# Thirty-two experts in a fixed order: the next gate ahead of the down projection, 512-column products, 64-row combining

## The chip, the core and the metric

The kernel runs on one core of one Trainium2 chip. The metric is the device time of one execution in microseconds (us). A core has a matrix engine (TensorE; PE in the profile, its weight loads PEld), a vector engine (VectorE, DVE), a scalar engine (ScalarE, ACT), GpSimd (POOL), a queue engine that here only issues transfers (SyncE, SP) and 16 DMA engines. Every engine runs its own instructions in order and waits on semaphores for the others. Matrix products are written to PSUM (eight banks, of 512 float32 in each of 128 partitions); everything else lies in SBUF, 128 partitions wide.

## What is computed

One layer of an encoder on 256 tokens of 1024 channels: a token mixer (two kinds of attention), a normalization, a mixture of experts with the four best of 32 experts for each token, and a second normalization. The change touches the experts and the last normalization:

```python
logits = xt @ w_router + b_router
top_vals, top_idx = lax.top_k(logits, TOP_K)          # 4 of 32
gates = softmax(top_vals)
# for each expert e, on the tokens that chose it:
hcat = xb @ w_up[e] + b_up[e]                         # 1024 -> 2048
gate = min(hcat[:, :1024], 7.0)
up = clip(hcat[:, 1024:], -7.0, 7.0)
act = gate * sigmoid(1.702 * gate) * (up + 1.0)
ys = act @ w_down[e] + b_down[e]                      # 1024 -> 1024
# out[token] += gate weight * ys;  x = layer_norm(alpha * x + out, ln2_g, ln2_b)
```

All is float32. The weights of the experts are 32 x 12 MiB, and each is read once.

## The kernel before, in words

The first 230 us are the mixer, the first normalization and the router. Then come the experts. An expert has room for 64 tokens, and two experts make a pair: `gather_x` picks the tokens of a pair with 0/1 matrices (`oh`) by TensorE products (tile `px`, line 575) and copies them, transposed, to `xe` (ACT, line 577).

An expert (`expert`, lines 596 to 656) is computed in two halves of 512 hidden channels. For each half, `up(c, 0)` makes the gate products and `up(c, 1)` the up products, each into one PSUM tile `pu` of 128 x 256 (two such tiles take turns). The two 64-row halves of `pu` hold two groups of 256 columns. A product starts with the bias, two bfloat16 matmuls (line 710), then come eight steps over the 1024 input channels (line 606). VectorE limits the gate (line 613), ScalarE takes the sigmoid (615), VectorE multiplies (616), limits the up part (619) and multiplies (620). `turned` transposes the result (line 626, tile `pa`, copied by ACT at 628), and `down` (line 636) multiplies it with the down weights into `pd`, whose two 64-row halves are 512 output columns each. ACT and DVE copy one half of `pd` each (653, 655) to `y`, at the rows of the expert within the pair.

When a pair is done, `combine` (line 681) multiplies the 128 rows of `y` with the gate weights `ot` and adds to four PSUM banks `acc`. `gates_of` makes `ot` (588 to 593). `start` puts the biases of the down projection (675) and the scaled residual (676) into `acc`, during expert 0.

The weights lie in memory as pieces of 1 MiB, 12 to an expert. `load` (lines 111 to 119) takes 20 places in SBUF in turn (`SLOTS`); SP issues all the loads in one queue, and a load waits until TensorE has read the place's former piece, and by a ring of eight semaphores for the landing of an earlier load. Ten pieces are loaded while the mixer runs. The last piece is loaded in two halves. Behind it SP loads the last normalization's two rows, spread to 128 partitions by the transfer (lines 734, 735).

A scheduler of the framework decides the order on each engine before the run; the order of the code is only its input.

Of the kernel before, what the change touches and what calls it, by code (L numbers as in the profile page):

```python
# [10 lines left out]
F32 = mybir.dt.float32  # L11
# [57 lines left out]
def encoder(ctx, tc, x, xt, w_in, b_in, lam, w_pa, w_pb, w_out, b_out, ln1g, ln1b, cols, b_r, w_ex, b_up,  # L69
# [39 lines left out]
    here = {}  # L109

    def load():

        n = len(here)
        e, j, h = n // 12, n // 2 % 6, n % 2
        r = slot(SLOTS[n % len(SLOTS)])
        here[e, j, h] = part(r, 0, 2048, 4 if j < 4 else 2)
        c = 1024 if n == 12 * NE - 1 else 2048
        for i in range(0, 2048, c):
            nc.sync.dma_start(r[:, i:i + c], w_ex[e, n % 12, :, i:i + c])

    def weights(e):
        while len(here) < 12 * (e + 1):
            load()
        return lambda c, b, k: here[e, 2 * c + b, k // 4][:, k % 4], lambda c, k: here[e, 4 + c, k // 2][:, k % 2]


    with ExitStack() as c1:
# [142 lines left out]
        def softmaxes(b, c, tabs):  # L270
# [9 lines left out]
            for j in range(2):  # L280
                p = turn("p", ps_)
                for tt in range(NT):
                    i = 2 * j + tt
                    s = moe.tile([P, T], F32, name="s", tag="gc", bufs=4)
# [77 lines left out]
        lamt = moe.tile([P, 4, HD], F32, name="lamt", tag="oh")  # L362
# [201 lines left out]
    def gather_x(ps, q, pos):  # L564

        oh = moe.tile([P, NT, 2, CAP], F32, name="oh", tag="oh")
# [3 lines left out]
        xe = moe.tile([P, KD, P], F32, name="xe", tag=f"xe{q % 2}")  # L570
        for k0 in range(0, KD, 4):
            px = ps.tile([P, 4, P], F32, name="px", tag="m")
            for k in range(4):
                for tt in range(NT):
                    PE.matmul(px[:, k], x1[:, tt, (k0 + k) * P:(k0 + k + 1) * P],  # L575
                              oh[:, tt].rearrange("p a b -> p (a b)"), start=tt == 0, stop=tt == NT - 1)
            S.copy(xe[:, k0:k0 + 4], px)  # L577
        return oh, xe

    def gather(ps, q, pos, g):  # L580
        oh, xe = gather_x(ps, q, pos)
        return xe, gates_of(ps, oh, g)

    def gates_of(ps, oh, g):
# [3 lines left out]
        V.tensor_mul(og, oh, g[:, :, :, None].to_broadcast(sh))  # L588
# [7 lines left out]
    def expert(ps, xe, i, wu, wd, bias, y, after=None):  # L596

        ats = []

        def up(c, b):  # L600
            pu = ps.tile([P, 256], F32, name="pu", bufs=2)
            for h in range(2):
                bias(pu[h * CAP:(h + 1) * CAP], b * FE + c * 512 + h * 256)
# [39 lines left out]
        if after is not None:  # L643
            after()
# [212 lines left out]
```

## Time and profile before

| | |
|---|---|
| median of 3 runs | 1199.31 us (1198.02 to 1201.79) |
| the profiled execution | 1198.99 us, of which the span of its instructions is 1197.2 us |
| TensorE busy in the span | 1103.0 us (92%) |
| VectorE, ScalarE, GpSimd busy | 304.3, 214.4, 54.5 us |
| read from memory | 439.2 MB |
| mean granted clock of TensorE | 0.99 of full speed |

The span runs from the first instruction of the profiled execution to its last; 1.8 us lie around it. Busy times of different engines overlap.

### The profile page before, as it was taken

The page shows a single profiled execution, that of the slowest core. Times are in us where ns is not written, and L with a number is a line of the kernel's source. Part 1 is how long each engine was busy: PE and PEld are TensorE (multiplying, and loading weights), DVE is VectorE, ACT ScalarE, POOL GpSimd, SP SyncE. Part 2 cuts the span into 40 slices and gives each one's busy share as a digit, 9 for nine tenths or more (in the row PEclk, how much of TensorE's full clock was granted, in tenths as well). Part 3 has the DMA queues.
Part 4 walks back from the last instruction along what each step waited for, and adds up shares of the span by engine and source line. Part 5 has one row for each costly group of instructions (what it writes and reads, how often), then busy time and mean ns, then how long its engine had stood idle before and what let it go on. Part 6 is the DMA issues. An engine that isn't in the chain of part 4 may idle for free.

```text
span 1197.2 us, 18167 instructions
## 1 busy us (share of the span) xinstructions
PE 1103.0 (92%) x7805; PEld 684.6 (57%) x7806; DVE 304.3 (25%) x698; ACT 214.4 (18%) x463; POOL 54.5 (5%) x77
## 2 busy tenths in 40 slices
PE   6989999899999999999989898989898989898985
PEld 6878999645555454545555555555554545455552
DVE  5857457411111111111111111111111111111113
ACT  4556654301010000000000000000000000000001
POOL 1720002100000000000000000000000000000001
PEclk9999999899999999999999999999999999999998
DMA  8765758689999999999999999999999999999951
GB/s 290 248 230 191 263 178 317 237 331 422 420 420 422 420 420 422 420 421 421 421 422 420 420 422 420 421 421 420 422 420 421 421 421 420 421 421 422 419 227 38
DMA packets 86951, 441.49 MB, mean 369 GB/s; under 512 B 7378, under 2 KB 33618, under 8 KB 37746
## 3 DMA queue, kind: packets, MB, share of 16 engines
q1 hardware_dynamic: 85954, 437.50, 90.2%
q0 software_dynamic: 720, 2.62, 0.7%
q8 instruction: 63, 1.03, 0.4%
q10 hardware_dynamic: 192, 0.16, 0.0%
q14 instruction: 22, 0.18, 0.0%
HBM read 439.20 MB, written 1.05 MB: 368 GB/s over the span
## 4 chain that ended last, share of the span: by engine, by line
PE 85%; DVE 8%; ACT 2%; DMA 2%; issue 2%; SPq 0%; POOL 0%; ACTq 0%; DVEq 0%
PE pu L606 38%; PE pd L636 19%; PE pt L206 7%; PE px L575 6%; PE acc L681 5%; PE pt L208 3%; PE pa L626 2%; DVE uc L620 2%; DVE uc L619 2%; DMA r_s<-in_w_in 1%; ACT xe L577 1%; DVE r_w L185 1%; DVE gc L613 1%; PE pu L710 1%; DVE y L655 1%
## 5 line engine op out<-in xcount | busy, mean ns | idle before, releaser
L206 PE MATMUL pt<-r_xh,r_w 128*128 128x256 f32 x512 | 98.9, 292 | 10.5 <-ACT r_w L184 5.8
L613 DVE TENSOR_SCALAR gc<-pu 128x256 f32<-128x256 f32 x64 | 27.1, 424 | 297.5 <-PE pu L606 297.5
L606 PE MATMUL pu<-r_a,xe 128*64 128x256 f32 x832 | 98.4, 381 | 0.0
L206 PEld LDWEIGHTS pt<-r_xh,r_w 128*128 128x128 f32 x512 | 83.1, 197 | 13.5 <-ACT r_w L184 5.5
L575 PE MATMUL px<-oh,x 128*128 128x128 f32 x512 | 77.7, 294 | 6.6 <-ACT xe L577 6.6
L655 DVE COPY y<-pd 64x512 f32<-64x512 f32 x32 | 22.0, 689 | 239.9 <-ACT y L653 130.7
L185 DVE TENSOR_TENSOR r_w<-r_s,r_w 128x512 fp32r<-128x512 f32 x104 | 72.4, 714 | 40.7 <-ACT r_w L184 40.3
L575 PEld LDWEIGHTS px<-oh,x 128*128 128x128 f32 x512 | 64.1, 195 | 32.1 <-issue 22.2
L606 PEld LDWEIGHTS pu<-r_a,xe 128*64 128x64 f32 x832 | 61.7, 137 | 32.0 <-issue 6.7
L184 ACT CAST r_w<-r_s 128x512 fp32r<-128x512 f32 x112 | 66.9, 617 | 62.0 <-PE pt L206 35.3
L710 PE MATMUL pu<-bupp,sel 96*64 96x256 bf16 x256 | 45.1, 285 | 35.7 <-DVE uc L619 20.6
L619 DVE TENSOR_SCALAR uc<-pu 128x256 f32<-128x256 f32 x64 | 27.2, 424 | 198.4 <-PE pu L606 198.4
L206 PE MATMUL pt<-r_xl,r_w 128*128 128x256 f32 x256 | 73.8, 288 | 0.0
L628 ACT COPY at<-pa 128x256 f32<-128x256 f32 x64 | 23.8, 372 | 274.0 <-PE pa L626 274.0
L615 ACT ACTIVATE sg<-gc 128x256 f32<-128x256 f32 x64 | 26.7, 417 | 230.6 <-DVE gc L613 230.6
L681 PE MATMUL acc<-y,ot 128*128 128x512 f32 x128 | 59.2, 605 | 5.5 <-DVE y L655 5.5
L710 PEld LDWEIGHTS <-sel 96*64 96x64 bf16 x256 | 25.3, 108 | 64.5 <-issue 56.8
L653 ACT COPY y<-pd 64x512 f32<-64x512 f32 x32 | 18.5, 579 | 198.1 <-DVE y L655 100.3
L636 PE MATMUL pd<-r_a,at 128*64 128x512 f32 x224 | 51.6, 597 | 0.0
L606 PE MATMUL pu<-r_w,xe 128*64 128x256 f32 x416 | 51.0, 382 | 0.0
L206 PEld LDWEIGHTS pt<-r_xl,r_w 128*128 128x128 f32 x256 | 50.5, 197 | 0.1
L606 PE MATMUL pu<-r_s,xe 128*64 128x256 f32 x416 | 50.5, 380 | 0.0
(236 smaller groups left out, 1509.9 us busy)
## 6 DMA issues: line engine op xcount, KB each, us to landing
r_a<-in_w_ex SPq DMA_DIRECT2D x79, 1024.0 KB, 16.4
r_s<-in_w_ex SPq DMA_DIRECT2D x38, 1024.0 KB, 16.7
r_w<-in_w_ex SPq DMA_DIRECT2D x38, 1024.0 KB, 15.7
r_s<-in_w_in SPq DMA_DIRECT2D x19, 1024.0 KB, 5.8
r_qa<-in_w_ex SPq DMA_DIRECT2D x19, 1024.0 KB, 15.0
r_tab<-in_w_ex SPq DMA_DIRECT2D x19, 1024.0 KB, 16.3
r_qb<-in_w_ex SPq DMA_DIRECT2D x19, 1024.0 KB, 16.3
r_v<-in_w_ex SPq DMA_DIRECT2D x19, 1024.0 KB, 17.0
```

What stands on the lines that cost most here:

```text
L184: S.copy(w[:, 0:2], src)
L185: (G if n % 4 == 3 and n >= 80 else V).tensor_sub(w[:, 2:4], src, w[:, 0:2].bitcast(F32))
L206: PE.matmul(os[j], w[:, a + b, c], d[:, k], start=st, stop=sp)
L208: PE.matmul(os[j], d[:, k, c], w[:, a + b], start=st, stop=sp)
L575: PE.matmul(px[:, k], x1[:, tt, (k0 + k) * P:(k0 + k + 1) * P], oh[:, tt].rearrange("p a b -> p (a b)"), start=tt == 0, stop=tt == NT - 1)
L606: PE.matmul(pu[h * CAP:(h + 1) * CAP], xe[:, k, i * CAP:(i + 1) * CAP], wu(c, b, k)[:, h * 256:(h + 1) * 256], start=False, stop=k == KD - 1)
L613: V.tensor_scalar(gc, pg, LIMIT, None, op0=ALU.min)
L619: V.tensor_scalar(uc, pu, LIMIT, -LIMIT, op0=ALU.min, op1=ALU.max)
L636: PE.matmul(pd[dh * CAP:(dh + 1) * CAP], at[:, j, h * CAP:(h + 1) * CAP], wd(c, k)[:, dh * 512:(dh + 1) * 512], start=c == 0 and j == 0 an ...
L655: V.tensor_copy(o, p)
L681: PE.matmul(acc[tt][dh], ot[:, tt], y[:, dh * 512:(dh + 1) * 512], start=False, stop=last)
L710: PE.matmul(o, sel[:, e:e + 1].to_broadcast([3 * NE, CAP]), bupp[:, c:c + 256], start=True, stop=False)
```

## The change

The weights are laid out in other pieces: four each of gate, up and down, each piece being two of the eight steps with all 1024 columns (`w_ex` is transposed so on the host). They are loaded in the order gate 0, up 0, and from then on gate e+1, down e, up e+1. A product is 512 columns wide into a PSUM bank of its own (`pg` for the gate, `pu` for up), so an expert has one gate and one up product in place of two each. The loop over experts runs the next expert's gate products before this expert's down products. The small work (gathering, transposing, gate weights, combining) is put between two steps of a product by `hooks`. Combining is done for each expert: `pd` keeps its two 64-row halves, ACT copies it whole to `y2`, and `routed` multiplies 64 rows. From the experts on, `manual_schedule` takes the order of the code as the order of each engine. The down biases and the residual are added after experts 15 and 17. The last normalization's rows are loaded to one partition by ScalarE's queue and spread to 128 by TensorE (`spread`), during expert 31's up product.

```diff
+    stream = [("g", 0), ("u", 0)]
+    for e in range(NE):
+        stream += [(("g", e + 1), ("d", e), ("u", e + 1)), (("d", e),)][e == NE - 1]
+    stream = [(b, e, m) for b, e in stream for m in range(4)]
...
-            nc.sync.dma_start(r[:, i:i + c], w_ex[e, n % 12, :, i:i + c])
+            nc.sync.dma_start(r[:, i:i + c], w_ex[e, 4 * "gud".index(b) + m, :, i:i + c])
...
+    def up(ps, tag, xe, i, w, bias, o, hooks=()):
+
+        pu = ps.tile([P, 512], F32, name="p" + tag)
+        hooks = dict(hooks)
+        for h in range(2):
+            bias(pu[h * CAP:(h + 1) * CAP], o + h * 512)
+        for k in range(KD):
             for h in range(2):
...
+                PE.matmul(pu[h * CAP:(h + 1) * CAP], xe[:, k, i * CAP:(i + 1) * CAP],
+                          w(k)[:, h * 512:(h + 1) * 512], start=False, stop=k == KD - 1)
+            if k in hooks:
+                hooks[k]()
+        return pu
...
+    def turned(ps, a):
+        pa = ps.tile([P, 4, P], F32, name="pa", tag="m")
+        for j in range(4):
+            PE.transpose(pa[:, j], a[:, j * P:(j + 1) * P], ident)
+        at = moe.tile([P, 4, P], F32, name="at", tag="at")
+        S.copy(at, pa)
+        return at
...
+        y = moe.tile([P, 512], F32, name="y2", tag="y2")
+        S.copy(y, pd)
         return y
+
+    def routed(o, tt, dh, ot, y, start, stop):
+        q = slice(dh * CAP, (dh + 1) * CAP)
+        PE.matmul(o, ot[q, tt], y[q], start=start, stop=stop)
...
+        ordered.enter_context(tc.manual_schedule())
...
+        gate_of(0, {3: counts})
+        up_of(0, {3: lambda: gates_for(0)})
+        for e in range(NE):
+            n = e + 1
+            nq = n // 2 + 1
+            more = n % 2 and nq < NE // 2
+
+            def first(n=n, nq=nq):
+                prepare(nq)
+                gather_half(ps, ohs[nq], xes[nq], 0)
+
+            if n < NE:
+                gate_of(n, {1: first, 5: lambda e=e: turn_of(e)} if more else {5: lambda e=e: turn_of(e)})
+            else:
+                S.activation(dummy, ots[e][:, 0, 0:1], AF.Sqrt, bias=epsc, scale=0.0)
+                turn_of(e)
+            down_of(e)
+            if n < NE:
+                hooks = {2: lambda e=e: combine(e), 6: lambda n=n: gates_for(n)}
+                if more:
+                    hooks[4] = lambda nq=nq: gather_half(ps, ohs[nq], xes[nq], 1)
+                if n == NE - 1:
...
+                    row = part(slot("tab"), 0, 2048, 2)[0:1]
+                    for j, src in enumerate((ln2g, ln2b)):
+                        S.dma_start(row[:, j], src[None, :])
+
+                    def spread(j, dh):
+                        pr = ps.tile([P, 512], F32, name="pr", tag="m")
+                        c = slice(dh * 512, (dh + 1) * 512)
+                        PE.matmul(pr, ones[0:1], row[:, j, c], start=True, stop=True)
+                        S.copy(rows2[:, j, c], pr)
+
+                    for k, a in zip((0, 1, 3, 4), ((0, 0), (0, 1), (1, 0), (1, 1))):
+                        hooks[k] = lambda a=a: spread(*a)
+                up_of(n, hooks)
+            if e == 15:
+                down_biases()
+            if e == 17:
+                residual()
+
+        combine(NE - 1)
```

What this does to the order shows first on TensorE in the middle of the experts. Before, at the end of an expert's up product (`pu` from piece `r_ob`; `sel` and `bupp` are the bias, `pa` the transposes of the result `uc`):

```order
L606 MATMUL pu<-r_ob,xe 64x256 x7
L710 LDWEIGHTS sel
L710 MATMUL pu<-bupp,sel 64x256 [waits DVE_49]
L710 LDWEIGHTS sel
L710 MATMUL pu<-bupp,sel 64x256
L626 MATMUL pa<-ident,uc 128x128 [waits DVE_49]
L626 MATMUL pa<-ident,uc 128x128
L606 MATMUL pu<-r_ga,xe 64x256 [waits DMAHW2_49]
```

Now the same engine in the gate product of the next expert (`pg`), with the transposes of the expert before (`pa`) put in ahead of the product's last two steps (piece `r_xl`), and the down product (`pd`) behind:

```order
L605 MATMUL pg<-r_xh,xe 64x512 [waits DMAHW4_49]
L605 MATMUL pg<-r_xh,xe 64x512 x3
L628 MATMUL pa<-ident,uc 128x128 [waits Activation_49]
L628 MATMUL pa<-ident,uc 128x128 x3
L605 MATMUL pg<-r_xl,xe 64x512 [waits DMAHW5_49]
L605 MATMUL pg<-r_xl,xe 64x512 x3
L637 MATMUL pd<-r_a_3111,at 64x512 [waits DMAHW6_49,Activation_49]
```

Before, a bias that needs VectorE and a transpose that needs it too stood directly behind the product whose result VectorE has to read; now a whole gate product less two steps stands between a product and its transposes, and four matmuls and more between the transposes and the down product.

The second place is the end, before, on SP's queue (`r_a` is the last weight's place, `r_qa` that of the normalization's rows):

```order
L119 DMA r_a_7576<-in_w_ex 128x2048 [waits DMAHW0_49,PE_49]
L119 DMA r_a_7578<-in_w_ex 128x1024 [waits DMAHW1_49,PE_49]
L119 DMA r_a_7578<-in_w_ex 128x1024 [waits DMAHW2_49]
L734 DMA r_qa<-in_ln_g 128x1024 [waits DMAHW3_49,PE_49]
L735 DMA r_qa<-in_ln_b 128x1024 [waits DMAHW4_49]
```

Now on ScalarE's queue (`y_6218` is the result of expert 30, `pr` the bank into which TensorE spreads a row):

```order
L640 COPY y_6218<-pd 128x512 [waits PE_49,Activation_49]
L753 DMA r_tab<-in_ln_g 1x1024 [waits DMAHW4_49,DMAHW0_49]
L753 DMA r_tab<-in_ln_b 1x1024 [waits DMAHW5_49]
L759 COPY r_qa<-pr 128x512 [waits DMAHW6_49,DMAHW2_49,PE_49]
L759 COPY r_qa<-pr 128x512 [waits PE_49] x3
```

The rows left SP's queue, where they stood behind the last weights, for ScalarE's, where they stand behind the copy of expert 30's result. Up to the experts the order of every engine is what it was, SP's up to its end as well.

## Rows read from the trace of the kernel before

**Rows 1.** The page: memory traffic in 40 equal slices of the span.

```profile
GB/s 290 248 230 191 263 178 317 237 331 422 420 420 422 420 420 422 420 421 421 421 422 420 420 422 420 421 421 420 422 420 421 421 421 420 421 421 422 419 227 38
```

**Rows 2.** Windows: span; busy of PE, PEld, DVE, ACT, POOL; clock; DMA share; GB/s.

```profile
235.00:255.00 20.00, 19.57 (x126) 9.71 (x122) 4.22 (x11) 1.21 (x3) 0.00 (x0) 1.00 0.98 411
255.00:262.00 7.00, 7.00 (x25) 2.31 (x26) 0.42 (x1) 0.37 (x1) 0.00 (x0) 1.00 0.14 34
...
273.90:329.58 55.68, 54.83 (x388) 30.63 (x390) 9.35 (x21) 5.48 (x12) 0.00 (x0) 1.00 1.01 421
300.00:1140.00 840.00, 783.67 (x5455) 433.24 (x5452) 130.61 (x296) 75.86 (x169) 0.00 (x0) 1.00 1.01 421
951.65:1011.70 60.05, 55.69 (x388) 30.74 (x390) 9.25 (x21) 5.38 (x12) 0.00 (x0) 1.00 1.01 421
1148.00:1160.00 12.00, 11.23 (x72) 4.92 (x68) 1.54 (x3) 0.95 (x2) 0.00 (x0) 1.00 0.47 191
```

**Rows 3.** Waits of PE from 400 to 1150 us: total, times, longest.

```profile
PE pu L710 <- DVE uc L619: 19.6, 38, 0.5
PE pu L710 <- DVE gc L613: 13.1, 25, 0.5
```

**Rows 4.** Waits of SP's queue over the span.

```profile
SPq L119 <- PE pu L606: 393.5, 205, 12.8
...
SPq L119 <- DMA r_a<-in_w_ex: 36.6, 22, 2.3
```

**Rows 5.** Timeline, start of the experts: start, us, engine, line, what.

```profile
231.14 1.08 PE L606 MATMUL pu<-r_a,xe 128*64 128x256 f32 x6
...
233.83 5.51 SPq L119 DMA_DIRECT2D r_a<-in_w_ex  x4
...
249.76 1.12 PE L675 MATMUL acc<-bdn,gatT 32*128 32x512 f32 x2
...
258.19 0.64 PE L636 MATMUL pd<-r_p,at 128*64 128x512 f32 x1
```

**Rows 6.** Timeline, the end of the span.

```profile
1133.70 6.10 SPq L119 DMA_DIRECT2D r_a<-in_w_ex  x5
...
1174.38 7.09 PE L636 MATMUL pd<-r_a,at 128*64 128x512 f32 x32
...
1181.51 0.68 DVE L655 COPY y<-pd 64x512 f32<-64x512 f32 x1 [7.62 <-PE pd L636]
...
1191.30 1.32 SPq L767 DMA_DIRECT2D out<-r_qb  x3
```

**Rows 7.** DMA issues: KB each, median us from issue to landing.

```profile
bcol<-in_cols ACTq DMA_DIRECT2D x1, 28.5 KB, 2.6
...
r_a<-in_w_ex SPq DMA_DIRECT2D x2, 512.0 KB, 15.8
...
r_qa<-in_ln_g SPq DMA_DIRECT2D x1, 512.0 KB, 15.0
```

**Rows 8.** Timeline of PE, one of each small piece between products.

```profile
29.25 1.14 PE L276 MATMUL sc<-r_qa 64*128 64x256 f32 x8
...
261.28 0.30 PE L710 MATMUL pu<-bupp,sel 96*64 96x256 bf16 x2
...
280.56 2.05 PE L575 MATMUL px<-oh,x 128*128 128x128 f32 x16
...
947.95 3.70 PE L681 MATMUL acc<-y,ot 128*128 128x512 f32 x8 [0.36 <-DVE y L655]
...
985.32 0.44 PE L626 MATMUL pa<-ident,uc 128*128 128x128 f32 x2 [0.16 <-DVE uc L620]
```

**Rows 9.** Groups by line: busy, mean ns of one, idle before.

```profile
L577 ACT COPY xe<-px 128x512 f32<-128x512 f32 x32 | 18.7, 585 | 167.9 <-PE px L575 167.9
```

**Rows 10.** Windows of 2 us where TensorE stood idle, columns as in group 2.

```profile
66.00:68.00 2.00, 0.00 (x0) 0.00 (x0) 2.00 (x4) 0.78 (x2) 1.64 (x3) 1.00 0.67 242
68.00:70.00 2.00, 1.90 (x9) 0.91 (x10) 0.65 (x2) 0.21 (x1) 0.57 (x1) 0.62 0.36 78
```

More of the change, by code (lines that the diff above doesn't have):

```diff
@@ new lines, in turned, with down @@
+    def turned(ps, a):
[5 more added lines that the diff above has]
+        return at
+    def down(ps, at, w):
+        pd = ps.tile([P, 512], F32, name="pd")
+        for k in range(KD):
+            for dh in range(2):
+                PE.matmul(pd[dh * CAP:(dh + 1) * CAP], at[:, k % 4, k // 4 * CAP:(k // 4 + 1) * CAP],
+                          w(k)[:, dh * 512:(dh + 1) * 512], start=k == 0, stop=k == KD - 1)
+        y = moe.tile([P, 512], F32, name="y2", tag="y2")
+        S.copy(y, pd)
+        return y
@@ L667, in start, with residual @@
             V.tensor_copy(gatT, gt[:NE].rearrange("e (a b) -> e a b", a=NT))
+            for tt in range(NT):
+                for dh in range(2):
+                    PE.matmul(acc[tt][dh], gatT[:, tt], bdn[:, dh * 512:(dh + 1) * 512], start=False, stop=False)
+        def residual():
             ai = moe.tile([P, P], F32, name="ai", tag="og")
             V.tensor_scalar(ai, ident, ALPHA, None, op0=ALU.mult)
-            bdn = moe.tile([NE, D], F32, name="bdn", tag="y")
-            S.dma_start(bdn, b_dn)
@@ L672, in start, with bias_of, bias @@
             for tt in range(NT):
                 for dh in range(2):
-                    c = slice(dh * 512, (dh + 1) * 512)
-                    PE.matmul(acc[tt][dh], gatT[:, tt], bdn[:, c], start=True, stop=False)
-                    PE.matmul(acc[tt][dh], ai, x1[:, tt, c], start=False, stop=False)
-        def combine(ot, y, last):
+                    PE.matmul(acc[tt][dh], ai, x1[:, tt, dh * 512:(dh + 1) * 512], start=False, stop=False)
+        def bias_of(e):
+            def bias(o, c):
+                PE.matmul(o, sel[:, e:e + 1].to_broadcast([3 * NE, CAP]), bupp[:, c:c + 512], start=True, stop=False)
+            return bias
@@ L679, in combine, with down_of, gates_for @@
+        def down_of(e):
+            ys[e] = down(ps, acts.pop(e), weights("d", e))
+        def gates_for(e):
+            ots[e] = gates_of(ps, ohs[e // 2], e % 2, gat[:, :, e])
+        def combine(e):
+            ot, y = ots.pop(e), ys.pop(e)
             for tt in range(NT):
                 for dh in range(2):
-                    PE.matmul(acc[tt][dh], ot[:, tt], y[:, dh * 512:(dh + 1) * 512], start=False, stop=last)
-        oh, xe = gather_x(ps, 0, posm[:, :, 0:2])
-        nxt = xe, None
@@ L733, in encoder @@
[L733 to L738 removed]
+                    routed(acc[tt][dh], tt, dh, ot, y, e == 0, e == NE - 1)
+        prepare(0)
+        for h in range(2):
+            gather_half(ps, ohs[0], xes[0], h)
@@ L769, in encoder @@
         final(acc)
+        ordered.close()
         most = nc.values_load(cnti[0:1, NE:NE + 1], min_val=0, max_val=T)
@@ L803, in bias @@
                     def bias(o, c):
-                        PE.matmul(o, ones[0:1, :CAP], bt[:, c:c + 256], start=True, stop=False)
+                        PE.matmul(o, ones[0:1, :CAP], bt[:, c:c + 512], start=True, stop=False)
                     for m, b0 in enumerate((CAP, 3 * CAP)):
```

225 lines of the change are left out of this document (82 added, 143 removed).

## The prediction, made before the changed kernel was run

> **What bounds the kernel now.** I first read the page's row of traffic: from slice 9 (270 us) to slice 37 it stands at 420 to 422 GB/s and never above [rows 1]. The windows say why that is a ceiling: the DMA share is 1.01 at 421 GB/s for 840 us [rows 2]. From 274 to 330 us TensorE got through a pair of experts in 55.68 us, which uses up 24 pieces of 1.0486 MB, or 452 GB/s, and the memory still gave 421 [rows 2]. So the faster consumption was lived from pieces loaded ahead.
>
> Then TensorE. In the steady part a pair takes 60.05 us, 55.69 of them busy [rows 2]; that is 25.17 MB / 60.05 us = 419 GB/s, as fast as memory delivers. But TensorE does not wait for memory there: of the 4.36 us idle, the waits from 400 to 1150 us are for VectorE, some 0.5 us each, at the bias behind a product whose result is still being read (32.7 us in these two rows alone) [rows 3]. The loads in turn wait for places that TensorE frees (393.5 us), and sometimes for the ring of eight (22 times on one place) [rows 4]. So two engines run side by side at the same pace, with about half of the places landed and unread between them.
>
> That stock is what the end shows. The last weight is issued at about 1139.4 (end of the row of five) and lands 15.8 us later, at 1155 [rows 6, 7]. TensorE ends the last product only at 1181.5, and from there it is 15.7 us to the end of the span at 1197.2 [rows 6]. The time is thus: last landing 1155.2, TensorE's remainder 26.3, tail 15.7, and 1.8 around the span, 1199.0 for the profiled execution, within 0.03% of the median.
>
> **The change part by part: TensorE's pace.** A pair keeps six products' worth of 32 matmul records; 512 columns instead of 256 change no sum, since the down product already has that form: 7.09 us each [rows 6], 42.5. Gathering: two times 16 records of 2.05, 4.1 [rows 8]. Transposes: 8 of the results and now 4 of the gate weights instead of 2, at 0.22, 2.6 [rows 8]. Biases: 4 of twice the width of the 0.30 row, 0.5 each, 2.0 [rows 8]. Combining: 64-row matmuls alternating between upper and lower rows stand in the scores of the attention, 8 records of 256 columns in 1.14 us [rows 8]; for 512 columns some 2.3, twice a pair, 4.6. Against this a pair's combining today is 3.70 [rows 8], so two unpaired ones would cost 7.4. The sum is 55.8 us a pair, and 58.6 with unpaired combining. These durations count each piece's run-out, which the next piece covers, so I take 53.5, with 52 and 58.6 as bounds. The trace's own pair without waits, 55.68 with 0.85 idle, has its matmuls in a less regular order [rows 2].
>
> The Trainium skill, page "TensorEngine Tiling (Array Packing)", section Key Properties, says that a change of tiling mode drains the engine; combining by 64 rows adds such changes. The 1.14 us row holds one entry into that mode, so a drain is in my 4.6.
>
> **Waits.** The 0.5 us waits go: gate, up and down have a bank each, and a product of another kind stands between a bank's reading and its next writing. What VectorE does next to it (limit and multiply, 128 x 512, about the 0.68 of the copy [rows 6] each, and the 0/1 matrix) has two steps, 1.7 us, before the first gathering needs it: 0 to 0.3 us a pair. The shared bank of gathering, transposing and gate weights is copied in 0.585 us [rows 9] with at least 1.7 us of product between two uses. Cover gone, each would cost about 0.5 us.
>
> **The stream.** Memory now sets the pace, as 25.17 MB / 421 GB/s is 59.8 us a pair against 53.5. Nothing in the experts lets it stop: before, it fell to a share of 0.14 from 255 to 262 us, because expert 0 held its places while TensorE put biases and residual into the banks, 249.76 to 258.19 [rows 2, 5]. That work, 8.4 us, now comes at experts 15 and 17 in two parts, and the places that are landed or free outlast it. The front is the same, so TensorE starts at 231.1 and frees the first place at about 233.8 [rows 5]. Forward: 364 MiB are left after the first 20 pieces; from 235.5 at 421 GB/s they take 906.6 us, end 1142. Backward: from 1155.2 off 6.0 for the gap, and 4.3 for the end, where 12 us moved 2.29 MB, of which 1.05 MB are the spread rows that leave [rows 2, 7]; 1145. I take 1144. At 422, the highest of the page's row [rows 1], it would be 1140; with the end as slow as before 1149.
>
> **TensorE after the last landing.** It starts 231.1 and needs 16 x 53.5 + 8.4, and four spreads; it has 20 pieces of stock, 50 us, and gains 6.3 us a pair, so it catches up around the ninth pair and from there follows the landings, 2.49 us a piece. The end, counted back from the last landing: expert 30's last down piece lands at -19.9, its product ends at -18.2, ACT copies 0.585 and issues the two rows. A transfer on ACT's queue took 2.6 us, one on SP's busy queue 15.0 [rows 7]; on its own queue I take the first. So the rows are there at -14.5, and expert 31's up product waits for them behind its first step. Behind that: seven steps of 0.86 (6.0), four spreads of a quarter of 3.70 (3.7), combining 2.1, gate weights 0.4: to -2.3. VectorE 1.4, four transposes 0.8, copy 0.6, five hand-overs of 0.1: +1.0. The down product 7.09: +8. Were the rows not in the way, TensorE would end at +2; with rows after 15.0 us, at +20.
>
> **The tail.** One copy on ACT replaces two in turn (0.7 less [rows 6]); combining is 1.4 shorter. Against it the two halves' statistics now stand in the order written, VectorE waits twice for ACT's root, and the four stores stand behind GpSimd's, where one went out early. Before, three were issued at 1191.30 [rows 6]. I take 16.4 instead of 15.7, bounds 14 and 17.5.
>
> Sum: 1144 + 8 + 16.4 + 1.8 = **1170 us**, 29 less: 11 by the stream, 18 by TensorE's remainder, 0.7 back.
>
> **The rivals.** *Rows late*: they land after 15.0 us as on SP's queue; +12, 1182. Against it: the other queue and one short line each. *TensorE stays the bound*: its last product ends at 231.1 + 8.4 + 4 + 16p, so the time, with the tail and 1.8 us, is 262 + 16p for p us a pair. It decides from p = 56.8; at 57.5 the time is 1182, at 58.6 it is 1200. For it: the sum of durations gives 55.8, unpaired combining 58.6; against it the paired row. *Slower*: the shared and single banks do make TensorE wait. There are six uses of the shared bank and six products a pair; 12 waits of 0.5 as in [rows 3] on 53 make 59, and 262 + 16 x 59 = 1206; it decides from p = 58.8. Against it: at least 1.7 us of product stands between. *The stream gains nothing*: it ends at 1155 as now, and only TensorE's remainder goes: 1181. For it: memory is at its ceiling already; against it the gap at 255.
>
> *The clock falls while TensorE waits for memory.* It fell to 0.62 behind an idle stretch from 66 to 68 us [rows 10]. In the last seven pairs TensorE would wait about 0.8 us at each piece, 12% in all, and the clock held at 1.00 with 7% idle [rows 2]. Were it at half, a step would take twice its time, TensorE would fall behind, stop waiting and be busy again, and only the 8 us after the last landing would double: 1178. The Trainium skill, page "TensorE: Matmul & The Clock Gate", section "HAM oscillation — how this bites in real kernels", tells of a kernel where each wait for memory let the clock fall; its waits were longer than the work between them, and here they are shorter.
>
> The Trainium skill, page "DMA: Bandwidth & Descriptors", section Specifications, puts the ceiling of the DMA fabric at 435 GB/s. The trace shows 421, 3% less, and by the page the stream would end near 1113; the trace decides.
>
> **How the numbers follow.** Forecast, memory-bound to the end: 0.66 (1157 to 1177). Rows late 0.10, TensorE the bound below 1196 0.08, clock 0.05, stream no earlier 0.04, slower 0.04, none of it and no change 0.03. Below 1157 is a little of the first. What the range has to hold reaches from 1157 to 1185. A measurement of this kernel tells a change from none at about 0.3%, 3.6 us: faster 0.91, same 0.04, slower 0.05.
>
> **What would show it.** Right: pairs of 53 to 54 us in the first half, later 59.8 with TensorE waiting for the weights' pieces; traffic at 421 without the gap after 255; the last weight landing near 1144; the first spread waiting for its row; the last down product ending 8 us behind the landing. Wrong: no wait for pieces anywhere, which means a pair above 56.8; traffic under 420 in the experts; a last product that ends more than 12 us behind the last landing.

## The result, and the profile of the changed kernel

The changed kernel takes **1182.41 us** (median of 4 runs, 1178.69 to 1182.79); the kernel before took 1199.59 us in its runs on the same chip. The ratio is 0.9849 with a 95% interval of 0.9823 to 0.9874: faster by 1.5%, where 2.4% had been forecast. The number is 12 us later than the forecast's likeliest value and above the 1157 to 1177 that the forecast itself was given; it lies inside 1157 to 1185, which was to hold the rivals too. The profiled execution took 1182.13 us, its span is 1180.4.

The page shows who sets the end now: the traffic in 40 slices, and the chain of work that ended last, of which transfers (DMA) hold 56%; before, TensorE held 85% of it and transfers 2%.

```profile
GB/s 283 260 228 200 253 161 319 227 412 421 421 421 420 421 421 421 421 421 421 421 421 421 421 421 422 422 421 421 421 421 422 421 421 421 421 421 421 421 323 38
...
DMA 56%; PE 22%; DVE 1%; issue 1%; ACT 0%; SPq 0%; ACTq 0%
```

In the windows (span; busy of PE, PEld, DVE, ACT, POOL; clock; DMA share; GB/s) the stop of the stream behind 255 us is gone: 423 GB/s where [rows 2] have 34. A pair of experts takes 53.05 us without any idle while there is stock (400 to 453), and 59.60 with 55.24 busy when there is none (587 to 647):

```profile
235.00:255.00 20.00, 19.99 (x106) 7.78 (x102) 4.76 (x12) 1.22 (x2) 0.00 (x0) 1.00 1.00 397
255.00:262.00 7.00, 7.00 (x35) 2.43 (x36) 1.72 (x3) 1.22 (x2) 0.00 (x0) 1.00 1.01 423
400.00:453.05 53.05, 53.04 (x262) 19.88 (x260) 7.39 (x13) 4.77 (x8) 0.00 (x0) 1.00 1.01 421
587.10:646.70 59.60, 55.24 (x264) 19.04 (x262) 7.39 (x13) 4.78 (x8) 0.00 (x0) 1.00 1.01 421
1120.00:1130.00 10.00, 7.82 (x36) 2.14 (x34) 1.72 (x3) 0.63 (x1) 0.00 (x0) 1.00 1.01 420
1130.00:1140.00 10.00, 6.64 (x16) 1.49 (x12) 0.00 (x0) 1.17 (x2) 0.00 (x0) 0.69 1.01 418
1140.00:1147.00 7.00, 7.00 (x19) 1.82 (x18) 0.00 (x0) 0.59 (x1) 0.00 (x0) 0.71 0.59 242
1147.00:1150.00 3.00, 3.00 (x11) 0.83 (x12) 0.00 (x0) 1.14 (x2) 0.00 (x0) 1.00 0.01 5
```

TensorE's regular waits for VectorE in the experts [rows 3] are gone. What is left of them is one of 1.5 us at the down biases, one of 1.7 at the residual and one of 1.6 ahead of the last down product. In their place TensorE waits some 0.5 us for single pieces (1.5 at the longest), and once 3.0 us for a row of the last norm (total, times, longest):

```profile
PE pd L637 <- DMA r_a<-in_w_ex: 3.9, 9, 0.5
PE pu L605 <- DMA r_w<-in_w_ex: 3.8, 9, 0.6
...
PE pr L758 <- DMA r_tab<-in_ln_g: 3.0, 1, 3.0
```

The timeline of the end shows that wait and what comes behind it. Expert 30's result is copied at 1130.22, ACT issues the row at 1130.30, TensorE stands from 1131.75 and goes on at 1134.77. From there four records of the up product take 1.98 instead of 1.08 us. The granted clock (1.00 is 2.4 GHz, 0.50 is 1.2) had fallen during the wait, as the second block shows, a window in which TensorE does nothing:

```profile
1129.95 0.39 PE L692 MATMUL pu<-bupp,sel 96*64 96x512 bf16 x2
...
1130.67 1.08 PE L605 MATMUL pu<-r_w,xe 128*64 128x512 f32 x4 [0.34 <-DMA r_w<-in_w_ex]
1134.77 2.04 PE L758 MATMUL pr<-r_tab,ones 1*128 1x512 f32 x2 [3.02 <-DMA r_tab<-in_ln_g]
1136.74 1.98 PE L605 MATMUL pu<-r_w,xe 128*64 128x512 f32 x4
...
1142.55 2.73 PE L645 MATMUL acc<-y,ot 64*128 64x512 f32 x8
1145.22 1.08 PE L605 MATMUL pu<-r_w,xe 128*64 128x512 f32 x4
...
1154.26 0.63 PE L628 MATMUL pa<-ident,uc 128*128 128x128 f32 x4 [1.61 <-DVE uc L622]
1155.62 7.09 PE L637 MATMUL pd<-r_a,at 128*64 128x512 f32 x32 [0.73 <-ACT at L630]
```

```profile
1134.00:1134.70 0.70, 0.00 (x0) 0.00 (x0) 0.00 (x0) 0.00 (x0) 0.00 (x0) 0.50 1.03 427
```

It is not the only fall in the experts. Behind expert 15 the clock is at half from 693.5 to 703.8 us, where the eight products of the down biases (over 32 rows) take 6.85 us:

```profile
693.16 6.85 PE L681 MATMUL acc<-bdn,gatT 32*128 32x512 f32 x8 [1.52 <-DVE gatT L678]
```

By the prediction's three terms: the last weight has landed at 1147 (traffic falls to 5 GB/s), where 1144 was forecast; TensorE's last product ends at 1155.62 + 7.09 = 1162.7, 15.7 us behind it, where 8 was forecast; from there to the end of the span are 17.7 us, where 16.4 was forecast. So 3, 7.7 and 1.3 us are missing, 12 in all. Against before (1155.2, 26.3, 15.7) the landing gave 8.2, TensorE's remainder 10.6, and the tail took 2.0 back.

### The profile page after: what moved, and what is told of

Read it like the earlier page. It is cut to its first block, busy times and chain, and to the rows that moved or that the text cites. A ratio compares the mean times of both kernels' runs of the same rounds, so it can differ in the third digit from the quotient of the medians.

```text
span 1180.4 us, 14053 instructions
## 1 busy us (share of the span) xinstructions
PE 1095.8 (93%) x5797; PEld 509.1 (43%) x5798; DVE 274.1 (23%) x570; ACT 206.3 (17%) x403; POOL 55.0 (5%) x77
## 4 chain that ended last, share of the span: by engine, by line
DMA 56%; PE 22%; DVE 1%; issue 1%; ACT 0%; SPq 0%; ACTq 0%
DMA r_a<-in_w_ex 10%; DMA r_xl<-in_w_ex 8%; DMA r_ob<-in_w_ex 8%; DMA r_s<-in_w_ex 7%; DMA r_v<-in_w_ex 7%; PE pg L605 6%; PE pu L605 6%; DMA r_w<-in_w_ex 5%; PE pd L637 5%; DMA r_gb<-in_w_ex 3%; DMA r_qb<-in_w_ex 3%; DMA r_p<-in_w_ex 3%; PE px L581 2%; PE acc L645 1%; PE acc L681 1%
## 5 line engine op out<-in xcount | busy, mean ns | idle before, releaser
L594 DVE COPY ot<-po 128x256 f32<-128x256 f32 x32 | 13.6, 424 | 508.5 <-PE po L592 508.5
L210 PE MATMUL pt<-r_xh,r_w 128*128 128x256 f32 x512 | 101.0, 296 | 10.5 <-ACT r_w L188 5.8
L583 ACT COPY xe<-px 128x512 f32<-128x512 f32 x32 | 18.8, 586 | 356.6 <-PE px L581 349.3
L613 DVE TENSOR_SCALAR gc<-pg 128x512 f32<-128x512 f32 x32 | 22.1, 692 | 246.0 <-PE pg L605 246.0
L645 PE MATMUL acc<-y,ot 64*128 64x512 f32 x256 | 64.3, 621 | 0.7 <-ACT y L640 0.7
L640 ACT COPY y<-pd 128x512 f32<-128x512 f32 x32 | 18.8, 586 | 214.0 <-PE pd L637 214.0
L605 PE MATMUL pg<-r_a,xe 128*64 128x512 f32 x224 | 53.2, 613 | 0.0
L605 PE MATMUL pu<-r_a,xe 128*64 128x512 f32 x192 | 46.3, 603 | 2.6 <-DMA r_a<-in_w_ex 2.6
L212 PE MATMUL pt<-r_w,r_xh 128*128 128x256 f32 x256 | 47.6, 285 | 0.7 <-DVE r_w L189 0.7
L212 PEld LDWEIGHTS pt<-r_w,r_xh 128*128 128x128 f32 x256 | 40.2, 192 | 2.1 <-DVE r_w L189 1.2
L645 PEld LDWEIGHTS acc<-y,ot 64*128 64x128 f32 x256 | 22.4, 189 | 43.0 <-issue 41.4
L212 PE MATMUL pt<-r_w,r_xl 128*128 128x256 f32 x128 | 36.3, 284 | 0.2 <-DVE r_xl L490 0.2
## 6 DMA issues: line engine op xcount, KB each, us to landing
r_a<-in_w_ex SPq DMA_DIRECT2D x79, 1024.0 KB, 19.8
r_s<-in_w_ex SPq DMA_DIRECT2D x38, 1024.0 KB, 19.8
r_w<-in_w_ex SPq DMA_DIRECT2D x38, 1024.0 KB, 19.8
r_qa<-in_w_ex SPq DMA_DIRECT2D x19, 1024.0 KB, 19.8
r_tab<-in_w_ex SPq DMA_DIRECT2D x19, 1024.0 KB, 19.8
r_qb<-in_w_ex SPq DMA_DIRECT2D x19, 1024.0 KB, 19.8
r_v<-in_w_ex SPq DMA_DIRECT2D x19, 1024.0 KB, 19.8
```

The costliest lines, as they stand in the source:

```text
L210: PE.matmul(os[j], w[:, a + b, c], d[:, k], start=st, stop=sp)
L212: PE.matmul(os[j], d[:, k, c], w[:, a + b], start=st, stop=sp)
L583: S.copy(xe[:, 4 * h:4 * h + 4], px)
L605: PE.matmul(pu[h * CAP:(h + 1) * CAP], xe[:, k, i * CAP:(i + 1) * CAP], w(k)[:, h * 512:(h + 1) * 512], start=False, stop=k == KD - 1)
L613: V.tensor_scalar(gc, pg, LIMIT, None, op0=ALU.min)
L640: S.copy(y, pd)
```

## The experiments

**Theory:** the largest miss, TensorE's remainder, is the wait for the late row and the half clock (0.50) behind it. **Rivals:** the spreads' one-row products lower the clock by themselves; or the waits for pieces do. Then, what the parts of the change are worth. All ratios are against runs of the kernel before on the same chip, whose medians lie between 1199.6 and 1200.9 us (so a microsecond between runs on different chips says nothing).

**1. The rows loaded early**, at expert 17, spreads left in place.

```
-                    row = part(slot("tab"), 0, 2048, 2)[0:1]
-                    for j, src in enumerate((ln2g, ln2b)):
-                        S.dma_start(row[:, j], src[None, :])
...
-                        PE.matmul(pr, ones[0:1], row[:, j, c], start=True, stop=True)
+                        PE.matmul(pr, ones[32 * j:32 * j + 1], rowt[32 * j:32 * j + 1, c], start=True, stop=True)
...
                 residual()
+                rowt = moe.tile([P, D], F32, name="rowt", tag="y")
+                for j, src in enumerate((ln2g, ln2b)):
+                    S.dma_start(rowt[32 * j:32 * j + 1], src[None, :])
```

> The two rows of the last norm are loaded at expert 17, into a place of their own, and TensorE's four spreads stay where they are, in expert 31's up product; only the wait for the late row goes. Theory (the 3.0 us wait for the row, and the half clock that came behind it until 1144, make TensorE's remainder 15.2 us where 8 was forecast): no idle stretch in the up product, the clock stays at 1.00 there, the last product ends about 7.7 us earlier, 1174 to 1176. Rival (the one-row products of the spreads lower the clock by themselves): only the 3.0 us of the wait come back, the up product still runs its steps at 2.0 us, 1179. Rival (waits for the weights' pieces lower it): the clock falls before the spreads too.

Measured: 1175.53 us (1172.82 to 1178.81), ratio 0.9791 [0.9772, 0.9810]. The timeline of TensorE has no wait for the row and steps of 1.08 us on both sides of the spreads:

```profile
1130.84 1.08 PE L605 MATMUL pu<-r_w,xe 128*64 128x512 f32 x4 [0.32 <-DMA r_w<-in_w_ex]
1131.84 1.12 PE L755 MATMUL pr<-rowt,ones 1*128 1x512 f32 x2
1132.89 1.08 PE L605 MATMUL pu<-r_w,xe 128*64 128x512 f32 x4
...
1148.29 8.74 PE L637 MATMUL pd<-r_a,at 128*64 128x512 f32 x32 [0.73 <-ACT at L630]
```

The theory's number and its rows; the one-row products and the waits for pieces leave the clock alone in this up product (run 10 has a fall among one-row products). But the last down product takes 8.74 us instead of 7.09, behind idle stretches that the changed kernel has too (to this, run 8).

**2. The spreads early as well**, in expert 31's gate product.

```
...
+                for k, a in zip((0, 2, 3, 4), ((0, 0), (0, 1), (1, 0), (1, 1))):
+                    gh[k] = lambda a=a: spread(*a)
             if n < NE:
-                gate_of(n, {1: first, 5: lambda e=e: turn_of(e)} if more else {5: lambda e=e: turn_of(e)})
+                gate_of(n, gh)
...
```

> Rows loaded at expert 17, and the four spreads moved from expert 31's up product to its gate product, which stands ahead of expert 30's down product: the path behind the last landing then holds none of them. Theory: another 3.7 us less than with the rows early alone if the up product was on the path, so about 1170 to 1172; TensorE's last product ends 5 to 8 us behind the last landing. Rival (the up product is not what sets the end once the wait is gone; the landing of the last down piece is): the same time as with the rows early alone.

Measured: 1172.57 us (1171.79 to 1173.18), ratio 0.9765 [0.9752, 0.9779]. Run 1 and this one differ by 3.0 us in their medians, and their intervals overlap a little; in the profiles the last product ends at 1153.6 instead of 1157.0. So the spreads were on the path, a little short of their 3.7 us. The last product ends 5.9 us behind the landing (1147.7), where 5 to 8 was expected.

**3. Only the wait.** As run 2, but expert 31's up product waits for a late row again, with products of one column.

```
+                    def touch():
+                        pr = ps.tile([P, 512], F32, name="pr", tag="m")
+                        for j in range(2):
+                            PE.matmul(pr[:, j:j + 1], ones[0:1], row[:, j, 0:1], start=True, stop=True)
+                    hooks[0] = touch
```

> As with the spreads early (rows at expert 17, spreads in expert 31's gate product), but the row is loaded late once more and two products of one column each wait for it in expert 31's up product, where the changed kernel waits. Theory (the idle wait by itself lowers the clock, and half of the loss is the clock's): 3 us idle, the steps behind it at 2.0 us until some 10 us later, 1178 to 1180. Rival (the clock fell because the wait was followed by one-row products): 3 us idle and steps at 1.0 us, 1175 to 1176.

Measured: 1177.96 us (1176.12 to 1181.61), ratio 0.9820 [0.9798, 0.9841]; 5.4 more than run 2.

```profile
1136.11 0.35 PE L768 MATMUL pr<-r_tab,ones 1*128 1x1 f32 x2 [3.98 <-DMA r_tab<-in_ln_g]
1136.78 0.38 PE L768 MATMUL pr<-r_tab,ones 1*128 1x1 f32 x2 [0.32 <-DMA r_tab<-in_ln_b]
1137.09 3.63 PE L605 MATMUL pu<-r_w,xe 128*64 128x512 f32 x8
1140.65 1.99 PE L645 MATMUL acc<-y,ot 64*128 64x512 f32 x8
```

4.3 us idle, and eight records in 3.63 instead of 1.89: the wait lowers the clock without the spreads behind it, as it did in the changed kernel before the first of them. The low stretch was shorter here, back at full clock at 1140.65, while the changed kernel had it until some 1144; its length is not the wait's alone.

**4. The rows by SyncE's queue**, that part of the change undone, no spreads.

```
...
+        nc.sync.dma_start(rows2[:, 0], bcast(ln2g, P, D))
+        nc.sync.dma_start(rows2[:, 1], bcast(ln2b, P, D))
```

> The part of the change on the last norm's rows undone: no spread by TensorE, the two rows go out by SyncE's queue to all 128 partitions behind the last weights, as in the kernel before; all else as after. Theory: 1.05 MB more behind the weights land some 5 to 16 us after the last weight and are needed some 20 us after it, so they cost nothing, and the wait, the half clock and the spreads go from TensorE: about 1170, 12 us less than the changed kernel. Rival (the spread transfer takes memory from the last weights and the last landing comes back to 1152 or later): 1178 or more.

Measured: 1174.09 us (1170.42 to 1175.26), ratio 0.9768 [0.9750, 0.9786], not to be told from run 2 and 8 us below the changed kernel. The rows' transfer, issued behind the last weight, cost nothing that these runs can show; taking it away, with a late row in its place, cost 8.

**5. Biases and residual in expert 0**, that part undone.

```
-        up_of(0, {3: lambda: gates_for(0)})
+        up_of(0, {3: lambda: gates_for(0), 5: down_biases, 6: residual})
...
-            if e == 15:
-                down_biases()
-            if e == 17:
-                residual()
```

> Down biases and residual go back to expert 0 (in its up product, with the banks opened there), all else as after. Theory (the stop of the stream at 255 us was worth what the traffic lost there, 6 us): the traffic falls again between 250 and 265 us, the last weight lands about 5 us later than 1147.5, and the time is 1186 to 1188. Rival (TensorE keeps a stock of landed pieces and what is put at expert 0 costs nothing, the end is TensorE's): within 1 us of 1182. Rival (it gains, since at expert 15 TensorE lost its clock over it for 10 us): below 1181.

Measured: 1191.39 us (1188.99 to 1191.82), ratio 0.9917 [0.9903, 0.9931]; 9.0 more than the changed kernel, more than the theory's 4 to 6. The windows:

```profile
235.00:255.00 20.00, 19.50 (x77) 6.29 (x74) 4.08 (x13) 2.72 (x6) 0.00 (x0) 0.94 0.88 351
255.00:265.00 10.00, 9.99 (x46) 4.54 (x46) 1.72 (x3) 0.59 (x1) 0.00 (x0) 0.96 0.50 197
265.00:285.00 20.00, 20.00 (x102) 7.79 (x98) 1.72 (x3) 1.80 (x3) 0.00 (x0) 1.00 0.97 390
1150.00:1157.00 7.00, 7.00 (x20) 1.76 (x19) 0.00 (x0) 0.77 (x2) 0.00 (x0) 0.75 0.49 205
```

Against 397, 422 and 422 GB/s in the changed kernel these three stretches lack 0.9, 2.2 and 0.6 MB, together 9 us of traffic. The first of them scatters between 351 and 411 in the runs that start the experts as the changed kernel does, so some 2 us of the 9 may be scatter. The end of the stream moves from 1147 to 1156, the time by the same 9. What stops the stream at its start is paid at its end, 900 us later.

**6. The fixed order undone**: the same pieces, sizes and banks, but the framework's scheduler places the experts' instructions.

```
-        ordered.enter_context(tc.manual_schedule())
```

> The fixed order alone undone: the same pieces, sizes and banks as after, but the framework's scheduler places the instructions of the experts on each engine (it moves the second product's biases and the first gathering of the start, the combining and the spreads). Theory (memory sets the pace from the middle on, and any order that keeps TensorE under 56.8 us a pair ends with the stream): within 6 us of 1182. Rival (the order is what keeps TensorE's pair at 53; without it waits of 0.5 us come back at the banks): pairs of 57 or more, 1190 or more.

Measured: 1244.34 us (1242.53 to 1245.33), ratio 1.0368 [1.0349, 1.0387]: slower than before. The theory (within 6 us of 1182) falls; the rival (pairs of 57 us or more, 1190 or more) holds. Three views: TensorE's waits; a window of one pair; and the group of the combining (busy, mean; in the changed kernel it is 64.3 us busy):

```profile
PE acc L645 <- ACT y L640: 20.1, 28, 0.7
PE pg L691 <- DVE gc L613: 19.8, 25, 0.8
PE pu L691 <- DVE uc L621: 19.0, 24, 0.8
PE po L592 <- ACT at L630: 9.8, 13, 1.0
PE px L581 <- ACT at L630: 7.3, 10, 0.7
```

```profile
587.10:650.70 63.60, 57.51 (x263) 20.91 (x261) 7.47 (x13) 4.78 (x9) 0.00 (x0) 1.00 1.01 416
```

```profile
L645 PE MATMUL acc<-y,ot 64*128 64x512 f32 x256 | 101.0, 637 | 20.1 <-ACT y L640 20.1
```

The pair takes 63.6 us, 10.6 more than in the fixed order: 6.1 idle, by the waits some 60% of it at the gate's and up's banks (L691) and the rest at the shared bank and for ACT's copy of the down result; and (101.0 - 64.3) / 16 = 2.3 more for combining, because the scheduler puts some of these products by themselves between the steps of the up product. What makes up the other 2 us was not followed up. The first two pairs, in which each combining still stands in one block, took 53.0 us each. With one bank a product, the new form of the experts needs its order; without it, it is the prediction's slower rival.

**7. No look-ahead**: gate, up and down of an expert one behind the other, still in a fixed order.

```
+    stream = [(b, e, m) for e in range(NE) for b in "gud" for m in range(4)]
...
+            turn_of(e)
+            down_of(e)
```

> The order of products undone alone: each expert's gate, up and down product one behind the other, weights loaded in that order, so TensorE stands idle for VectorE and ACT between up and down (in the profile after, at the last expert, 1.61 and 0.73 us, 2.3 an expert, 4.7 a pair). Theory (the time is the later of memory's and TensorE's ends, and TensorE is the later from 56.8 us a pair): pairs of 57.7 us, and 262 + 16 x 57.7 with the rows' 8, 1190 to 1200; more if the clock falls in these idle stretches. Rival (memory at 59.6 us a pair covers it): 1180 to 1185.

Measured: 1195.56 us (1193.52 to 1197.74), ratio 0.9964 [0.9948, 0.9980]. The waits and a window:

```profile
PE pa L625 <- DVE uc L619: 49.9, 31, 1.6
PE pd L634 <- ACT at L627: 23.3, 32, 0.7
```

```profile
300.00:500.00 200.00, 183.62 (x896) 68.66 (x896) 24.85 (x44) 16.09 (x27) 0.00 (x0) 0.99 1.01 421
```

A pair is 57.9 us by the starts of its down products, and 262 + 16 x 57.9 + 8 = 1196: at this pair the time follows TensorE, which waits for no piece at all. Undoing the look-ahead costs 4.9 of the 7.0 us that the change took off a pair; what the other 2.1 come from was not tried. The waits of 1.6 and 0.7 us stand ahead of all 32 down products here. The clock fell behind three of them, at 365, 956 and 1167 us, and the mean of 0.99 in the window is the first of these:

```profile
365.86 5.10 PE L634 MATMUL pd<-r_w,at 128*64 128x512 f32 x16 [0.73 <-ACT at L627]
```

Without a fall sixteen records take 3.60 us; the other 29 down products ran at full clock.

**8. Filler**: as run 2, with products that nobody reads in the two waits ahead of the last down product.

```
+                fill(3)
                 turn_of(e)
+                fill(1)
             down_of(e)
```

> The kernel with the spreads early, and four products whose results nobody reads: three of 512 columns while TensorE would wait 1.6 us for VectorE behind the last up product, one while it waits 0.7 us for ACT's copy. Theory (the last down product takes 8.6 to 8.8 us in four of the runs, against 7.09 in the changed kernel, because the clock falls behind these idle stretches): it holds at 1.00, the last down product takes 7.1, 1171. Rival (the fall has to do with what lay before, or with the instant, and not with these two waits): 8.6 again, 1172.6; rival (the four products come out longer than the waits): 1173 or more.

Measured: 1172.50 us (1168.94 to 1174.27), ratio 0.9768 [0.9747, 0.9790]: no change against run 2.

```profile
1140.92 2.84 PE L725 MATMUL pg<-x,ident 128*128 128x512 f32 x6
1143.61 0.60 PE L628 MATMUL pa<-ident,uc 128*128 128x128 f32 x4
1144.04 1.02 PE L725 MATMUL pg<-x,ident 128*128 128x512 f32 x2
1144.99 7.09 PE L637 MATMUL pd<-r_a,at 128*64 128x512 f32 x32
```

The down product takes 7.09, but the filler came out longer than the waits: the product starts 4.0 us behind the up product's end instead of 3.0, so 1.0 of the 1.5 us gained is spent. Behind the same two waits without filler it ran at full clock in five kernels' profiles (the changed one, runs 5, 6, 11 and 12) and took 8.62 to 8.78 in six (runs 1 to 4, 7 and 9); with it 7.09 in both that had it. So these waits can let the clock fall and need not; that filler prevents it is not shown by two profiles.

**9. The tail's order**: as run 2, both halves' statistics ahead of the roots' results, GpSimd's part stored by ACT's queue.

```
-                V.reciprocal(rs, rs)
...
+            for rs in rss:
+                V.reciprocal(rs, rs)
...
-                nc.sync.dma_start(out[tt * P:(tt + 1) * P, c], o)
+                if (tt, i) != (0, 1):
+                    nc.sync.dma_start(out[tt * P:(tt + 1) * P, c], o)
+            S.dma_start(out[:P, 512:], fo[:, 0, 512:])
```

> The kernel with the spreads early, and in the tail VectorE takes both halves' statistics before it waits for ACT's roots, and the store of the part that GpSimd finishes goes by ACT's queue instead of ahead of the other three on SyncE's. Theory (the tail, 17.7 us where 16.4 was forecast, holds two waits of VectorE for a root, some 0.7 us each, and stores that wait for GpSimd): about 1 us less than the 1172.6 with the spreads early, 1171 to 1172. Rival (the stores' landing sets the end, whatever their order): 1172.6.

Measured: 1171.15 us (1168.39 to 1172.44), ratio 0.9757 [0.9739, 0.9776]. The intervals overlap with run 2's; in the profile the last product ends at 1150.61 and the span at 1166.6, a tail of 16.0 us instead of 17.7.

**10. Filler and tail together.**

> Both: filler products and the tail's order. If the two gains are independent, 1169 to 1170.5; if the stores or the last weight's landing set the end, 1171 to 1172.6.

Measured: **1168.86 us** (1167.08 to 1170.09), ratio 0.9737 [0.9719, 0.9754]; the fastest of all, 13.6 us below the changed kernel. Which of its two parts carries it beyond run 2 these medians don't separate; the tail's 16.0 us are there again (1151.13 to 1167.1). Its profile also has a fall of the clock that no wait precedes: in expert 31's gate product, with the one-row spreads between its steps, TensorE had been busy for 17.4 of the 18 us from 1100 to 1118, with no wait above 0.6 us:

```profile
1116.37 1.08 PE L605 MATMUL pg<-r_oa,xe 128*64 128x512 f32 x4
1117.38 1.19 PE L750 MATMUL pr<-rowt,ones 1*128 1x512 f32 x2
1118.51 1.98 PE L605 MATMUL pg<-r_oa,xe 128*64 128x512 f32 x4
```

The same gate product kept its clock in the profiles of runs 2, 3, 8 and 9.

**11. Combining with its loops exchanged**, lower rows' two products first, then the upper rows'.

```
-            for tt in range(NT):
-                for dh in range(2):
+            for dh in range(2):
+                for tt in range(NT):
```

> As the changed kernel, but the combining's eight 64-row products run first the four of the lower rows' two banks and then those of the upper (loops exchanged), so that they no longer alternate between upper and lower rows. Theory (alternation is what lets two run at once): a combining of 3.4 us as in the run with the free order instead of 1.99, pairs of 55.9 us, still below 56.8, so the stream still ends it: within 3 us of 1182. Rival (64-row products overlap in any order, and what cost more in the free order was products between them): 1.99, pairs of 53.05. By the sum TensorE the bound: 262 + 16 x 55.9 + 8 = 1164, below the stream's.

Measured: 1184.17 us (1182.38 to 1186.30), ratio 0.9868 [0.9848, 0.9888], not told from the changed kernel. One combining of this run:

```profile
454.38 2.00 PE L645 MATMUL acc<-y,ot 64*128 64x512 f32 x8
```

It takes what it took before the exchange, and the pair 53.06: the theory that alternation is needed falls. In the run with the free order, where the scheduler splits the same eight records, two of them alone take as long as four:

```profile
594.88 1.12 PE L645 MATMUL acc<-y,ot 64*128 64x512 f32 x2 [0.73 <-ACT y L640]
595.93 1.94 PE L605 MATMUL pu<-r_pt,xe 128*64 128x512 f32 x8
597.80 1.13 PE L645 MATMUL acc<-y,ot 64*128 64x512 f32 x4
```

So products of the two halves overlap as long as they stand in one block, in either order, and not across other products.

**12. Half of the down weights left out**: two of the four pieces are loaded and each is used twice, so the result is not the reference's; TensorE's work is the same.

```
-    stream = [(b, e, m) for b, e in stream for m in range(4)]
+    stream = [(b, e, m) for b, e in stream for m in range(2 if b == "d" else 4)]
```

> Leaves out half of each expert's down weights: two pieces instead of four are loaded and each is used twice, so memory has 20 pieces a pair to bring (49.8 us at 2.49) instead of 24, and TensorE's work is the same. Theory (TensorE's own pace is 53 us a pair and memory is the bound of the changed kernel): no waits for pieces, pairs of 53 us to the end, and 256.8 + 31 x 26.5, 18 for biases and residual, 8 for rows and spreads, 7 for the last product and 19 behind it, about 1125 to 1135. Rival (the middle's 59.6 us a pair are TensorE's, by its clock or by its order): 1165 or more.

Measured: 1117.47 us (1115.43 to 1119.92), ratio 0.9311 [0.9288, 0.9334]. The window shows TensorE without idle and memory below its 421:

```profile
500.00:1060.00 560.00, 556.76 (x2692) 207.50 (x2690) 75.87 (x136) 48.34 (x81) 0.00 (x0) 0.99 0.94 376
```

Pairs are 53.05 us all the way, but for the two with the down biases and the residual (61.9 and 58.5). The end is 8 us below the estimate, which had counted a long wait for the late row; the last weight had landed by 1050 us, long before the row was issued at 1074.3, and the wait is 0.67 us. TensorE could end 65 us earlier than it does: in the changed kernel memory is the bound.

## Why the prediction was right, and where its numbers were off

The mechanism that was forecast is there: pairs of 53 us, then of 59.6 with waits for pieces, traffic at 421 GB/s without the gap, a wait for the row, an end behind the last landing. One of the prediction's own signs of being wrong is there too: the last product ends 15.7 us behind the last landing, where more than 12 was to count against it. The time by itself tells little, since four of the rivals had been priced at 1178 to 1182. The traces tell them apart: the row took 4.4 us and not 15.0, TensorE was not the bound, the stream ended 8 us earlier, and the clock fell, but not for the reason that its rival named. That the sum of three misses comes to the 12 us of *rows late* is chance.

**TensorE's pace: right.** 53.5 forecast, 53.05 measured; the sum of durations had been 55.8, and what the next piece covers was taken off. Combining is 1.99 for eight records where 2.3 was estimated; splitting a block (run 6) costs. The Trainium skill, page "TensorEngine Tiling (Array Packing)", section Key Properties, says that a change of mode drains TensorE; no run here prices that by itself. The rival that TensorE stays the bound needs a pair above 56.8: run 7, at 57.9, ends where the formula puts it. In run 6 the formula with 63.6 for all pairs would give 1280 where 1244 was measured; its first pairs were faster. In run 12, at 53.05, it gives 1111, 6.7 us below the measured time: the term of 8.4 for the down biases and the residual was too small. Their two pairs cost 8.9 and 5.4 us more than the others, 14.3 together, by waits of 1.5 and 1.7 us and the half clock behind expert 15. In the changed kernel memory hides that.

**Waits: right, and they are the order's.** The 0.5 us waits [rows 3] are gone because each shared bank has a product between its uses. Take the order away and waits of 0.8 us are there (run 6). The prediction's slower rival, bank waits at 59 us a pair, was real in its mechanism; what keeps it out is the order alone.

**The catching-up: wrong in time, without effect.** Forecast for the ninth pair, measured in the sixth (the pair from 522 us on). The stock of 20 places counted those still under way: a piece takes 19.8 us from issue to landing (the page's median), so the eight of the ring have not landed. An estimate from that is 12 places, some 30 us, which at 6.6 us a pair last 4.5 pairs; the first wait for a piece, at 528 us, comes 5.6 pairs after the start at 231.

**The stream: the mechanism right, its end mis-sized.** The forecast's "4.3 for the end" took the slow traffic of the last 12 us [rows 2] for the spread rows' doing. The rows are gone and the slow end is still there: 242 GB/s from 1140 to 1147, 1.69 MB that at 421 would take 4.0 us and take 7. Those are the 3 us between 1144 and 1147. The prediction had named the other case, 1149 with the end as slow as before. The gap behind 255 us, put at 6.0, is worth 7 to 9 (run 5), since its recovery is slow too; that is about the whole gain of the landing, 8.2.

**TensorE's remainder: the mis-sized term, 15.7 for 8.** "The rows are there at -14.5", by 2.6 us from issue to landing, was off (its own terms, -18.2 + 0.585 + 2.6, give -15.0): TensorE had its row 4.4 us after the issue (1130.30 to 1134.7), 12.3 us ahead of the last landing. That is 2.2 of the 7.7. The 2.6 came from a transfer at 0.8 us of the span, with memory at 43 GB/s (0 to 3 us); here it ran at 422. The other 5.5 us came behind the row: 28.0 to the last product's end, where 22.5 had been forecast. The wait itself had been forecast; that it would lower the clock was put at nothing, though [rows 10] show a fall behind an idle stretch. The up product ran until about 1144 at half level, four steps and spreads at some 2.0 instead of 1.0 us and most of a combining. Runs 1 and 3 show that the wait does it, and that without it the remainder is 9.8 us, of which 1.7 are the slow down product, so 8.1 for the forecast's 8. The clock rival had named the waits for pieces. These did nothing: 0.5 us each, at 93% busy from 587 to 647 us and at 78% from 1120 to 1130, clock 1.00 and no step at half level. The Trainium skill, page "TensorE: Matmul & The Clock Gate", section "HAM oscillation — how this bites in real kernels", tells of waits longer than the work between them that lowered the clock each time. The trace agrees for the 3.0 us wait, behind 1.08 us of work, and for the short waits for pieces. It doesn't account for every fall here: run 10's came without such a wait.

**The tail: 17.7 for 16.4.** Both causes were named ahead, VectorE's waits for the roots and stores behind GpSimd's, and priced too low together: run 9, which changes just these, has 16.0 us.

## What to carry to other kernels

When two engines run at one pace, find out which of them is the bound behind each change: here TensorE's 12% only moved the end as far as the stream allowed, and what the stream lost at the start of the experts came back 900 us later. A small transfer that becomes an operand near the end belongs far ahead of it: saving 1 MB of hidden traffic cost a wait, a clock fall and 8 us. And single banks with a fixed order go together: the same pieces in another order were 62 us slower.

## What the runs showed of the hardware

- An idle stretch of TensorE of 3 to 4 us near the end was followed by steps at the 1.2 GHz level in each of four profiles (the changed kernel, runs 3, 5 and 11). Shorter ones were followed by it at times: the waits of 1.6 and 0.7 us ahead of the last down product in six of the eleven profiles that have them, and the same waits ahead of all 32 down products in run 7 three times.
- The length of a wait does not decide alone. In the changed kernel a wait of 1.7 us at the residual (755 us) and one of 1.5 for a piece (between 900 and 1000 us) left the clock at 1.00. But in all twelve kernels that put the eight 32-row products of the down biases in one block, the clock fell during them or within 1 us of their end, with 1.5 us of wait ahead of them or, in runs 5 and 7, 0.5. In the kernel before and in run 6, where other products stand between them, it did not. Run 10's fall stood among one-row products. That few rows are the reason is not shown: no run changed the rows alone.
- The stream ends at about half its rate: 200 to 250 GB/s over the last 6 to 7 us in the changed kernel and in run 5, with the DMA share at half as well, and 222 from 1149 to 1157 in the kernel before. It doesn't where memory was below its ceiling to the last, in runs 6 and 12. What holds it back was not tried.
- A 4 KB row on ACT's otherwise empty queue took 4.4 to 4.6 us to its reader while memory ran at its ceiling (the changed kernel, runs 3, 5 and 11), and 1.5 us where the weights' stream was over or at its end (runs 7 and 12).
- One 64-row product alone takes as long as two on opposite halves (1.12 and 1.13 us), and four in a block take 1.99.
